# First tokens turned by the tensor engine, and score banks shared by two row tiles, in a hybrid attention layer

## Chip, cores and metric

The kernel runs on one core of one Trainium2 chip. The metric is the time of one execution in microseconds of device time; three runs of the kernel before are known.

## The reference

One layer for 2048 prompt tokens and 64 sample tokens with model width 1024. Only what the change touches is shown whole; the cache, the sample tokens and the output side are left out.

```
mod = silu(c) @ w_ada + b_ada                    # 1024 x 3072
shift, scale, gate = split(mod, 3)
h = rms_norm(x, norm_g) * (1 + scale) + shift
u = h @ w_in                                     # 1024 x 4104, split into q, k, v, z of heads A and B, f of B
qa, ka = rope(rms_norm(..)); qb, kb = rms_norm(..); logf = log_sigmoid(fb + b_f)
A: softmax(qa ka^T / 8, mask of 64-token chunks), two maps per head, a = p1 - lam * p2, a @ va
B: softmax(qb kb^T / 8 + cumulative logf bias, causal mask) @ vb
y = x + gate * (concat(A * silu(za), B * silu(zb)) @ w_out)
```

## The kernel before

**Tiling.** A block `j` is 256 tokens, two row tiles `t` = 0, 1 of 128 (row tile `i` = 2j + t); there are eight blocks and the sample block. The columns of `w_in` are cut into eight groups `g` of 512 columns, taken in the order 0, 1, 4, 5, 6, 7, 2, 3. Every product is done with operands split into an f16 high part and an f16 low part, and so costs three matmuls. `inp` computes the projection of one group and row tile (matmuls `q<-wc,hT`; `wc` are the split weights, `hT` the split and turned `h`, features on partitions). `q_evac`, `ep_*` normalise and rotate; `ep_trans` turns q and k (`tr<-ident,u`); `qk_pair` makes scores (`S<-KT,qT`); `qk_chunk` drains a score tile to `E` on VectorE; `row_*` make the softmax row and split it into `PB`; `row_trans` turns it by a DMA (`PT<-PB`); `pv` multiplies it with the values (`po<-VT,PT`).

**Start.** SP, the only queue that issues DMAs, first loads the weights of group 0 (`wc`, 2 MB), then the shift and scale columns of `w_ada` in sixteen 512 KB pieces (`wada`) with the two row tiles of block 0 (`x`) among them, then the weights of group 1. `mod_mm(hf, k)` multiplies the conditioning vectors with `wada`, first all of columns half 0, then half 1; it fills two column groups of the PSUM tile `modp`. `mod_evac` writes the result to `modr`, `mod_max` takes its maxima (`hb`), from which `sigma` makes the power of two `sig_h` that scales `h` before its split. `mod_rows` spreads `modr` over 128 partitions by matmuls, `h_first` and `h_first_split` compute and split `h` of block 0 on VectorE and ScalarE (`hl`), and `h_first_trans` turns it by four DMA transposes to `hT`. Later blocks do the same through `h_make`, `h_split` and `h_trans`, with shift and scale read back from DRAM into `shP` and `gsP`. The weights of a group are scaled by a power of two as well: `w_max` takes maxima per k (`wmx`), `w_peak` the maximum per partition, and `spread` writes the 128 numbers to DRAM (`wmx_d`) and reads them back into every partition (`wrow`); group 0 alone does this with two small matmuls (`all_max_mm`). `w_split` then makes `wc`. `warm` issues matmuls whose result nobody reads.

**Scores.** PSUM holds two score tiles `S` of 128x1024 (two banks each), one for each head of a group. `qk_pair(g, j, t, ci)` takes both for one row tile, multiplies 64-row halves of the array side by side, and adds the mask with matmuls over all 128 rows. Row tiles 0 to 3 need at most 512 columns.

**Order.** Every call is recorded with a position (`plan.event`, `ev`); `Plan` then orders the instructions of each engine: among those that could start about now it takes the one with the lowest priority number, which comes from positions, durations that the planner assumes (`cost`) and the table `SHIFT` (nanoseconds added for a kind of operation, one column for each ninth of the program). An event with `first` set goes ahead of all others. Engines run in that order and wait for each other by semaphores; a waiting instruction holds all behind it on its engine. All instructions are issued from one helper line (551).

Of the kernel before, what the change touches and what calls it, by code (L numbers as in the profile page):

```python
# [28 lines left out]
D = 1024  # L29
# [12 lines left out]
class Plan:  # L42
# [18 lines left out]
        'ep_apply DVE': (26127, -3870, -4149, 1952, -17698, -3554, -10514, -7088, -2181),  # L61
        'ep_gain POOL': (1598, 5296, 4273, 7950, 5296, 20643, 60755, 9385, 5296),
        'ep_hi ACT': (27471, 36841, 2957, 36442, -76347, -50798, 24757, 21188, 0),
        'ep_kout SP d': (-2090, 62103, 69083, 15305, -17069, 20450, 62522, 47446, -52402),
        'ep_lo DVE': (13690, 20015, 10272, -25398, 50409, 18413, 30933, 55598, 0),
        'ep_rstd POOL': (124196, -7418, -3334, -13672, 1489, -2852, -6964, -8380, 2958),
        'ep_square ACT': (1222, 7059, 69075, 100316, 33946, 17761, -559, 7791, -55499),
        'ep_square DVE': (-19737, -11205, -6053, -6235, 13891, -12021, 5467, -9194, -18777),
        'ep_square SP d': (17731, 2644, -20421, 44685, -453, 17057, 7365, -5250, -5933),
        'ep_trans PE': (-8510, 1413, 20757, 14554, 4162, -22993, -38513, -7700, 0),  # L70
        'ep_v ACT': (77357, 78843, 94474, 106969, 15393, 26795, 14839, 59051, 0),
        'ep_v DVE': (123205, 212871, 14149, 83229, 170299, 16014, -443, 779, 0),
        'f_evac ACT': (0, 283107, 0, 0, 0, 0, 0, 0, 0),
        'f_evac DVE': (0, 28121, 0, 0, 0, 0, 0, 0, 0),
        'first h0 ACT': (-47637, 0, 0, 0, 0, 0, 0, 0, 0),
        'first h0 DVE': (39992, 0, 0, 0, 0, 0, 0, 0, 0),
        'first h0 SP d': (-43600, 0, 0, 0, 0, 0, 0, 0, 0),
        'first h1 ACT': (20737, 0, 0, 0, 0, 0, 0, 0, 0),
        'first h1 DVE': (-3029, 0, 0, 0, 0, 0, 0, 0, 0),
        'first h1 SP d': (-3083, 0, 0, 0, 0, 0, 0, 0, 0),  # L80
        'first w ACT': (-1750, 0, 0, 0, 0, 0, 0, 0, 0),
        'first w DVE': (2329, 0, 0, 0, 0, 0, 0, 0, 0),
        'first w PE': (-14065, 0, 0, 0, 0, 0, 0, 0, 0),
        'first w POOL': (14606, 0, 0, 0, 0, 0, 0, 0, 0),
        'first x ACT': (-27378, 0, 0, 0, 0, 0, 0, 0, 0),
        'first x POOL': (148021, 0, 0, 0, 0, 0, 0, 0, 0),
# [9 lines left out]
        'gate_out ACT': (0, 0, 2849, 0, 0, 0, 0, 0, 0),  # L96
        'gate_out SP d': (0, 0, 77357, 0, 0, 0, 0, 0, 0),
        'gate_scale DVE': (0, 0, 0, 0, 0, 0, 0, 942, 38016),
        'h_load SP d': (-15270, 27231, 30875, 38614, 21795, -15328, 60179, -34016, 0),
        'h_make DVE': (1250, 15290, 0, 0, 0, 0, 0, 0, 0),  # L100
        'h_split ACT': (4400, 7716, 0, 0, 0, 0, 0, 0, 0),
        'h_split DVE': (-6743, 49591, 0, 0, 0, 0, 0, 0, 0),
        'h_stat ACT': (57185, -1335, 0, 0, 0, 0, 0, 0, 0),
        'h_stat POOL': (39, -11037, 0, 0, 0, 0, 0, 0, 0),
        'h_trans SP d': (2336, -121, 0, 0, 0, 0, 0, 0, 0),
        'inp PE': (-1425, -2353, -5892, 12276, 1110, 7213, 10417, 4982, 0),
        'mod ACT': (84262, 0, 0, 0, 0, 0, 0, 0, 0),
        'mod DVE': (-41547, 0, 0, 0, 0, 0, 0, 0, 0),
# [16 lines left out]
        'q_evac_s ACT': (0, 263668, 272342, 280051, 232653, 247574, 249782, 256882, 0),
        'q_evac_s DVE': (0, -32432, -42172, 30926, 8537, -46465, -66220, 99044, 0),
        'qk_chunk DVE': (-656, 14962, 14438, 14179, 33823, 12070, -8423, 32451, 24882),
        'qk_pair PE': (-686, -14880, -13186, -13282, -18376, -10584, -4934, 6105, -20805),
        'row_a_A DVE': (-4545, 35845, 81899, 0, 0, 0, 26630, 42209, 14393),
        'row_exp ACT': (239808, 30341, 63612, 112050, 254971, 49109, 107780, -3600, 161122),  # L130
        'row_hi_A ACT': (13875, -16282, 7088, 0, 0, 0, 4986, -3720, -18827),
        'row_hi_B ACT': (0, 0, 28449, 24237, 42298, 974, -14079, 0, 0),
        'row_lo_A DVE': (6455, -1845, 64402, 0, 0, 0, 42405, 45153, 41582),
        'row_lo_B DVE': (0, 0, 43352, 8756, 25691, 6871, 2028, 0, 0),
        'row_recip ACT': (5844, -78, 117755, 0, 0, 0, -69669, -12634, 71923),
        'row_recip DVE': (24207, 11431, 58294, 12857, 195542, 14343, 52846, 17171, -54082),
        'row_trans SP d': (-4043, 2148, 584, -10112, -3739, 584, 26131, 26487, 584),
        'second x ACT': (54758, 0, 0, 0, 0, 0, 0, 0, 0),
        'second x POOL': (-40204, 0, 0, 0, 0, 0, 0, 0, 0),
        'second x SP d': (-25850, 0, 0, 0, 0, 0, 0, 0, 0),  # L140
        'small ACT': (6570, 0, 0, 0, 0, 0, 0, 0, 0),
        'small DVE': (-1560, 0, 0, 0, 0, 0, 0, 0, 0),
        'small POOL': (1716, 0, 0, 0, 0, 0, 0, 0, 0),
        'small SP d': (39808, 0, 0, 0, 0, 0, 0, 0, 0),
        'smp_P ACT': (0, -75170, -26194, -12198, -25045, 28140, -35406, -31008, -38883),
        'smp_P PE': (0, -27764, -15612, -15612, -15612, -15612, -15612, -15612, -62941),
        'smp_PV PE': (0, -11187, -11670, 25841, 5585, -9507, -14440, -53633, -6031),
        'smp_S ACT': (0, -37793, -20363, -38036, 18373, 47712, -26322, 4578, -39853),
# [8 lines left out]
        'start ACT': (-58233, 0, 0, 0, 0, 0, 0, 0, 0),
        'start DVE': (47985, 0, 0, 0, 0, 0, 0, 0, 0),
        'start PE': (19278, 0, 0, 0, 0, 0, 0, 0, 0),
        'start SP d': (-2135, 0, 0, 0, 0, 0, 0, 0, 0),  # L160
        'w_coef DVE': (-9072, -20222, -33332, -11355, 19956, -7748, 16067, 0, 0),
# [1765 lines left out]
```

## Time and profile before

| | |
|---|---|
| three runs | 1624.32, 1626.23, 1629.85 us; median 1626.23 us |
| profiled execution | 1624.04 us, of it a span of 1622.3 us |
| PE busy | 1441.1 us (89%) |
| DVE (VectorE) busy | 1261.6 us (78%) |
| ACT (ScalarE) busy | 928.9 us (57%) |
| POOL (GpSimd) busy | 495.6 us (31%) |
| first matmul of the projection | 70.31 us after the span's start |

Busy time is time in which an instruction of the engine runs; a wait of PE is told with what released it. The clock columns give the granted clock of TensorE as a share of 2.4 GHz.

### The profile page before, as it was taken

To read this page: it belongs to the slowest core of one execution; us is meant where nothing else is said; L and a number is where in the kernel's file an instruction comes from. 1 tells how busy PE (TensorE), PEld (TensorE's weight loads), DVE (VectorE), ACT (ScalarE), POOL (GpSimd) and SP (SyncE) were. 2 spreads that over 40 slices of the span, in tenths; PEclk is the share of its full clock that TensorE was granted. 3 is DMA by queue.
4 is the path that set the end of the run, shared out by engine and by line. 5 is a ranking of instruction groups with operands and counts; after the bars stand their busy time and mean duration, and the time that the engine had idled before them with its cause. 6 is when DMAs were issued, how large, how long until landed. Compare 5 with 4: busy or idle time off the path is not lost. (4 is left out here: it accounts for less than half of the span.)

```text
span 1622.3 us, 29643 instructions
## 1 busy us (share of the span) xinstructions
PE 1441.1 (89%) x10900; PEld 729.1 (45%) x10900; DVE 1261.6 (78%) x2619; ACT 928.9 (57%) x1768; POOL 495.6 (31%) x620
## 2 busy tenths in 40 slices
PE   7499987888999988998889889988999899698998
PEld 3144444443454444444444444444444454344443
DVE  4588999978969886988678867986899789797431
ACT  2257765655567665775667656865665566453100
POOL 0056663324322121111212112112355354412322
PEclk9699999989999999999999999999999999899999
DMA  9758789957978899999999999999858664889772
GB/s 314 127 156 195 198 186 233 157 110 178 208 152 175 199 201 208 199 212 209 217 164 210 196 197 215 206 192 203 204 151 153 132 156 124 159 168 231 199 196 70
DMA packets 630414, 298.50 MB, mean 184 GB/s; under 512 B 513183, under 2 KB 601007, under 8 KB 623484
## 3 DMA queue, kind: packets, MB, share of 16 engines
q1 hardware_dynamic: 630268, 296.61, 85.1%
q8 instruction: 85, 1.39, 0.4%
q14 instruction: 61, 0.49, 0.1%
HBM read 129.12 MB, written 43.16 MB: 106 GB/s over the span
## 5 line engine op out<-in xcount | busy, mean ns | idle before, releaser
L551 PE MATMUL q<-wc,hT 128*128 128x512 f16 x3072 | 733.4, 383 | 27.3 <-DMA hT<-hl 17.3
L551 PEld LDWEIGHTS <-hT 128*128 128x128 f16 x3328 | 293.8, 98 | 336.6 <-issue 31.8
L551 ACT ACTIVATE E<-E,st 128x128 f32<-128x128 f32 (+15 forms) x256 | 305.9, 1196 | 158.7 <-DVE st L551 80.6
L551 PE MATMUL po<-VT,PT 128*128 128x128 f16 x3808 | 247.7, 215 | 82.3 <-DMA PT<-PB 44.6
L551 PEld LDWEIGHTS <-PT 128*128 128x128 f16 x3808 | 213.3, 100 | 154.1 <-DMA PT<-PB 69.2
L551 PE MATMUL S<-KT,qT 64*128 64x512 f16 (+3 forms) x1920 | 227.2, 355 | 17.8 <-DVE E L551 14.8
L551 DVE SCALAR_TENSOR_TENSOR PB<-E,PB 128x128 f16<-128x128 f32 (+15 forms) x128 | 164.2, 1298 | 33.7 <-ACT PB L551 32.9
L551 PE MATMUL y<-wc,ogT 128*128 128x512 f16 (+1 forms) x800 | 177.1, 380 | 2.5 <-DVE os_e L551 1.3
L551 POOL TENSOR_SCALAR rs<-rs 128x8 f32<-128x8 f32 (+1 forms) x72 | 20.6, 285 | 518.4 <-DVE rs L551 491.9
L551 ACT ACTIVATE PB<-E 128x128 f16<-128x128 f32 (+15 forms) x128 | 138.3, 1102 | 46.3 <-DMA PT<-PB 45.7
L551 DVE CUSTOM_DVE_ANT_0 E<-S,nk,cf 128x1024 f32<-128x1024 f32 (+7 forms) x128 | 131.5, 1045 | 42.6 <-PE S L551 42.4
L551 PEld LDWEIGHTS <-qT 64*128 64x128 f16 x1920 | 83.9, 95 | 143.6 <-issue 77.4
L551 DVE TENSOR_SCALAR_CACHE_REDUCE E<-S,cf 128x1024 f32<-128x1024 f32 (+7 forms) x128 | 131.4, 1042 | 13.0 <-PE S L551 12.7
L551 POOL TENSOR_TENSOR u<-u,gain 128x512 f32<-128x512 f32 (+1 forms) x72 | 96.1, 1335 | 98.1 <-DVE u L551 23.7
L551 POOL TENSOR_TENSOR rs<-rs,mhalf 128x8 f32<-128x8 f32 (+1 forms) x72 | 118.3, 1643 | 6.0
L551 PEld LDWEIGHTS <-ogT 128*128 128x128 f16 (+1 forms) x800 | 75.8, 98 | 95.9 <-issue 10.9
L551 ACT ACTIVATE u<-q,us 128x384 f32<-128x384 f32 x128 | 73.1, 572 | 75.4 <-PE q L551 37.3
L551 ACT ACTIVATE PB<-E,st 128x128 f16<-128x128 f32 (+7 forms) x64 | 76.6, 1198 | 41.1 <-DVE E L551 14.3
L551 DVE SCALAR_TENSOR_TENSOR PB<-E,st,PB 128x128 f16<-128x128 f32 (+8 forms) x64 | 87.6, 1369 | 9.7 <-ACT PB L551 9.4
L551 POOL TENSOR_TENSOR yt<-yt,xr 128x512 f32<-128x512 f32 (+1 forms) x34 | 44.0, 1295 | 142.4 <-DVE yt L551 116.0
L551 POOL TENSOR_SCALAR oar<-oar 128x1 f32<-128x1 f32 (+1 forms) x68 | 38.2, 562 | 155.6 <-ACT og L551 152.7
L551 ACT ACTIVATE og<-po,us 128x128 f32<-128x128 f32 x128 | 45.9, 359 | 60.9 <-PE po L551 51.5
(210 smaller groups left out, 1778.8 us busy)
## 6 DMA issues: line engine op xcount, KB each, us to landing
hT<-hTd SPq DMA_DIRECT2D x53, 1024.0 KB
out_dram<-u SPq DMA_DIRECT2D x128, 128.0 KB
wc<-in_w_in_dram SPq DMA_DIRECT2D x32, 256.0 KB
wada<-in_w_ada_dram SPq DMA_DIRECT2D x16, 512.0 KB
x<-in_x_prompt_dram SPq DMA_DIRECT2D x16, 512.0 KB
hTd<-hT SPq DMA_DIRECT2D x16, 512.0 KB
ogd<-og SPq DMA_DIRECT2D x64, 128.0 KB
nk<-nck_d SPq DMA_DIRECT2D x16, 512.0 KB
```

The costliest lines, as they stand in the source:

```text
L551: fn(*a, **kw)
```

## The change

1. `w_ada` is loaded in full rows k by k (eight times 1 MB) and not by column halves. `mod_mm(k)` issues four matmuls per k, into four column groups of `modp`; `mod_evac` takes all 128 partitions with one multiply-add and one maximum.
2. `h` of block 0 is turned by TensorE: ScalarE scales x by its row's reciprocal norm, sixteen f32 transposes turn it into the score tiles, and for each k VectorE applies shift and scale, now one number per partition (`mcol`, made by four transposes of `modr`), ScalarE writes the high part to `hT` and VectorE the low part. The four DMA transposes, the `mod_rows` matmuls and `hl` of block 0 go.
3. Group 1 takes its weight maximum by `all_max_mm` too, so its write to DRAM and the read back go.
4. `qk_pair` of blocks 0 and 1 makes the scores of both row tiles in one visit, in different banks of the same pair of `S` tiles.
5. `warm` matmuls are placed anew (88 at the start in the place of 90, and none of the twelve later ones), and the whole `SHIFT` table and two assumed durations are new, so that the order differs on every engine.

```diff
     SHIFT = {
-        'ep_apply DVE': (26127, -3870, -4149, 1952, -17698, -3554, -10514, -7088, -2181),
+        'ep_apply DVE': (28748, 396, -4145, 6923, -16510, 21685, -12270, -8722, -27945),
...
+    def load_ada(k):
...
+            t = st([128, 2, D], F32, f"wada{k}", tag=tag, bufs=bufs)
+            sp.dma_start(out=t.rearrange("p s c -> p (s c)"), in_=wada_v[:, k, 0:2 * D])
...
-        if g:
+        if g > 1:
             spread(g, m)
...
-        if g == 0:
-            all_max_mm(mod_ps["S0"][:, 512:1024], m[:, 0:1], m[:, 1:2])
+        if g < 2:
+            all_max_mm(O_tile() if g else mod_ps["S0"][:, 512:1024], m[:, 0:1], m[:, 1:2])
...
+        for hf in range(2):
+            for s in range(2):
+                c = 32 * (2 * hf + s)
+                pe.matmul(mod_ps["p"][c:c + 2, :], cs[:, k, :], ada_w[k][s][:, hf * 512:hf * 512 + 512], start=False, stop=(k == KC - 1))
+
+    def mod_evac():
+
+        dve.scalar_tensor_tensor(out=modr, in0=mod_ps["p"], scalar=mod1, in1=grow, op0=ALU.add, op1=ALU.mult)
+        dve.tensor_reduce(out=hb[:, 0:1], in_=modr, axis=AX, op=ALU.max, apply_absolute_value=True)
+
+    def mod_cols():
+
+        c = mod_ps["c"] = Q_tile("modc")
+        for q in range(4):
+            pe.transpose(c[:, q * 128:q * 128 + 128], modr[:, q * 128:q * 128 + 128], ident)
...
-        sp.dma_start_transpose(out=hT[0, 0][:, 8 * hf:8 * hf + 8, t * 128:(t + 1) * 128],
-                               in_=hhl[0, t][:, 4 * hf:4 * hf + 4].rearrange("p k a b -> p (k a b)"))
...
+    def h_first_x(t):
+
+        x = x_t[0, t]
+        act.activation(out=x, in_=x, func=AF.Copy, scale=hrs[0, t][:, 1:2])
+        for k in range(KC):
+            c = k % 4 * 256 + t * 128
+            pe.transpose(mod_ps[f"S{k // 4}"][:, c:c + 128], x[:, k * 128:k * 128 + 128], ident)
+
+    def h_first(k):
...
+        dve.tensor_scalar(out=x, in0=p, scalar1=mcol[:, 1, k:k + 1], scalar2=mcol[:, 0, k:k + 1], op0=ALU.mult, op1=ALU.add)
+        act.activation(out=hi, in_=x, func=AF.Copy)
+        dve.tensor_tensor(out=lo, in0=x, in1=hi, op=ALU.subtract)
...
+    for k in range(KC):
+        plan.event(-79.5 + 0.1 * k, True, "first h")
+        h_first(k)
...
+        ts = (0, 1) if j < 2 else (t,)
+        if t not in ts[:1]:
+            return
...
+    def S_cols(s, j, t):
+        return S_ps[s][:, 512 * t:512 * t + 512] if j < 2 else S_ps[s]
```

On SP, at the end of the loads, the kernel before has these rows (`wm_1` is the weight maximum of group 1, `hl_0` the split `h` of row tile 0):

```order
L551 DMA wmx_d_85<-wm_1_200 128x1
L551 DMA x_167<-in_x_prompt_dram 128x1024
L551 DMA shP<-mod_d 128x1024
L551 DMA wrow_201<-wmx_d_85 128x128
L551 DMA_TRANSPOSE hT_0_176<-hl_0_175 128x8x128 x2
L551 DMA gsP<-mod_d 128x1024
```

and the changed kernel these (`x_173` is block 1):

```order
L547 DMA mod_d<-modr 2x512 x4
L547 DMA wc_120<-in_w_in_dram 128x4x128
L547 DMA x_173<-in_x_prompt_dram 128x1024 x2
L547 DMA shP<-mod_d 128x1024
L547 DMA gsP<-mod_d 128x1024
L547 DMA x_0_239<-in_x_prompt_dram 128x1024
```

The write and read of the maxima and the transposes are gone from between the loads, and `gsP` is loaded directly behind `shP`.

On VectorE, the changed kernel has these rows where the last low part of block 0 is done and the maximum of group 1 (`wm_1`, with the matmuls into `po`) is still to be made; before, the maximum was read from `wrow`:

```order
L547 TENSOR_TENSOR hT_0_172<-x_1_153,hT_0_172 128x256 x2
L547 TENSOR_REDUCE wmx_199<-wc_115 128x1
...
L547 TENSOR_REDUCE wmx_199<-wc_120 128x1
L547 TENSOR_REDUCE wm_1_200<-wmx_199 128x1
L547 SCALAR_TENSOR_TENSOR x_173<-x_173,hr_0_175,gsP 128x1024
L547 TENSOR_REDUCE wm_1_200<-po 1x1
L547 TENSOR_TENSOR x_173<-x_173,shP 128x1024
L547 COPY wm_1_200<-po 128x1
```

Six of the eight `w_max` of group 1 now stand behind the first `h`, and the two passes over x of block 1, which read `gsP` and `shP`, stand between the steps of the maximum.

On TensorE, the changed kernel makes the scores of both row tiles of block 0 in one piece (the first visit of group 0; `S_0_0` and `S_0_1` are the two tiles):

```order
L547 MATMUL S_0_0_0_231<-KT_0_221,qT_0_222 128x128
L547 LDWEIGHTS qT_0_222
L547 MATMUL S_0_1_0_232<-KT_0_221,qT_0_222 128x128
L547 LDWEIGHTS qT_0_222
L547 MATMUL S_0_0_0_231<-KT_0_221,qT_0_222 128x256
L547 LDWEIGHTS qT_0_222
L547 MATMUL S_0_1_0_232<-KT_0_221,qT_0_222 128x256
...
L547 MATMUL S_0_1_0_232<-mask_b_100,ident_b 128x64
L547 LDWEIGHTS hT_1_216
L547 MATMUL q_1_0_224<-wc_126,hT_1_216 128x512
```

Before, the 128-column and the 256-column scores stood in two visits with projection matmuls between them; behind the one visit now come the last four k of a projection.

## Rows read from the trace of the kernel before

**Rows 1.** Busy time by stretch: us, then engines, clock, DMA share, GB/s.
```profile
14.00:38.00 24.00, 21.14 (x101) 7.03 (x99) 16.59 (x33) 7.84 (x13) 2.40 (x12) 0.94 1.04 389
38.00:42.00 4.00, 4.00 (x11) 0.52 (x12) 0.69 (x1) 0.00 (x0) 0.00 (x0) 0.50 1.06 235
54.00:66.00 12.00, 0.96 (x3) 0.58 (x3) 7.16 (x18) 3.82 (x6) 0.74 (x2) 0.50 0.80 41
70.00:80.00 10.00, 9.69 (x50) 4.12 (x51) 6.79 (x29) 4.66 (x8) 0.00 (x0) 0.68 0.79 168
```

**Rows 2.** Timeline of the SP queue: start us, length us, what.
```profile
28.39 0.37 SPq L551 DMA_DIRECT2D wada<-in_w_ada_dram  x1
54.89 0.35 SPq L551 DMA_DIRECT2D wmx_d<-wm  x1
55.82 0.37 SPq L551 DMA_DIRECT2D shP<-mod_d  x1
63.01 0.32 SPq L551 DMA_DIRECT2D wrow<-wmx_d  x1
63.42 5.73 SPq L551 DMA_TRANSPOSE hT<-hl  x2
```

**Rows 3.** Timeline of PE from the modulation to block 1.
```profile
38.60 8.79 PE L551 MATMUL modp<-wada,cs 128*2 128x512 f32 x30
54.01 0.37 PE L551 MATMUL mod<-ident,hb 128*2 128x128 f32 x1 [4.08 <-DVE hb L551]
70.31 1.03 PE L551 MATMUL q<-wc,hT 128*128 128x512 f16 x2 [14.49 <-DMA hT<-hl]
95.78 0.66 PE L551 MATMUL tr<-ident,u 128*128 128x128 f32 x4 [0.68 <-POOL u L551]
96.35 0.59 PE L551 MATMUL q<-wc,hT 128*128 128x512 f16 x2
```

**Rows 4.** Timeline of PE's weight loads in the modulation.
```profile
18.29 0.08 PEld L551 LDWEIGHTS modp<-bada,ones 1*2 1x2 f32 x2 [0.21 <-issue]
19.23 0.09 PEld L551 LDWEIGHTS modp<-wada,cs 128*2 128x2 f32 x2 [0.86 <-issue]
...
26.27 0.09 PEld L551 LDWEIGHTS modp<-wada,cs 128*2 128x2 f32 x2 [0.34 <-issue]
26.69 0.09 PEld L551 LDWEIGHTS modp<-wada,cs 128*2 128x2 f32 x2 [0.34 <-issue]
```

**Rows 5.** Timeline of VectorE, 53 to 98 us.
```profile
53.98 0.69 DVE L551 TENSOR_REDUCE wmx<-wc 128x1 f32<-128x512 f32 x1
56.23 0.22 DVE L551 TENSOR_SCALAR sig_h<-sig_h_e 128x1 int32<-128x1 int32 x2
69.25 0.29 DVE L551 TENSOR_REDUCE wm<-wrow 128x1 f32<-128x128 f32 x1 [7.94 <-DMA wrow<-wmx_d]
80.43 0.75 DVE L551 SCALAR_TENSOR_TENSOR wc<-wc,us,wc 128x512 f16<-128x512 f32 x1 [1.36 <-ACT wc L551]
85.22 1.28 DVE L551 SCALAR_TENSOR_TENSOR x<-x,hr,gsP 128x1024 f32<-128x1024 f32 x1
92.03 0.68 DVE L551 TENSOR_TENSOR u<-u,rs 128x512 f32<-128x512 f32 x1
97.26 0.48 DVE L551 SCALAR_TENSOR_TENSOR KT<-tr,sg,KT 128x256 f16<-128x256 f32 x1
```

**Rows 6.** Timeline of PE around a visit of `qk_pair` with 256 columns.
```profile
125.47 0.38 PE L551 MATMUL q<-wc,hT 128*128 128x512 f16 x1
125.77 0.50 PE L551 MATMUL S<-KT,qT 64*128 64x256 f16 x6
126.21 0.23 PE L551 MATMUL S<-mask_b,ident_b 128*128 128x64 bf16 x2
126.28 0.60 PE L551 MATMUL q<-wc,hT 128*128 128x512 f16 x2
126.71 0.20 PE L551 MATMUL qf<-wc,hT 128*128 128x16 f16 x2
```

**Rows 7.** Waits of PE from 100 us on: total, times, longest.
```profile
PE po L551 <- DMA PT<-PB: 44.6, 32, 6.1
PE S L551 <- DVE E L551: 14.8, 14, 7.5
```

More of the change, by code (lines that the diff above doesn't have):

```diff
@@ L157 @@
[L157 to L161, printed above, removed]
-        'w_coef POOL': (11122, 0, 0, 0, 0, 10141, 9150, 0, 0),
-        'w_load SP d': (1568, -13268, -10100, 20125, 22689, -53853, 40583, 0, 0),
-        'w_max DVE': (6726, 82742, 70908, 125915, -40677, -24609, 23494, 0, 0),
@@ new lines @@
+        'first h DVE': (-3578, 0, 0, 0, 0, 0, 0, 0, 0),
+        'first w ACT': (-58489, 0, 0, 0, 0, 0, 0, 0, 0),
+        'first w DVE': (166953, 0, 0, 0, 0, 0, 0, 0, 0),
+        'first w PE': (14802, 0, 0, 0, 0, 0, 0, 0, 0),
+        'first w POOL': (-10121, 0, 0, 0, 0, 0, 0, 0, 0),
+        'first x ACT': (888, 0, 0, 0, 0, 0, 0, 0, 0),
+        'first x PE': (459, 0, 0, 0, 0, 0, 0, 0, 0),
+        'first x POOL': (-11545, 0, 0, 0, 0, 0, 0, 0, 0),
[9 rows of a table added]
+        'gate_out ACT': (0, 0, 44671, 0, 0, 0, 0, 0, 0),
@@ new lines @@
+        'second x ACT': (57333, 0, 0, 0, 0, 0, 0, 0, 0),
+        'second x POOL': (-36654, 0, 0, 0, 0, 0, 0, 0, 0),
+        'second x SP d': (-37489, 0, 0, 0, 0, 0, 0, 0, 0),
+        'small ACT': (85370, 0, 0, 0, 0, 0, 0, 0, 0),
+        'small DVE': (-900, 0, 0, 0, 0, 0, 0, 0, 0),
+        'small POOL': (88770, 0, 0, 0, 0, 0, 0, 0, 0),
+        'small SP d': (67896, 0, 0, 0, 0, 0, 0, 0, 0),
+        'smp_P ACT': (0, -130836, -160843, -170685, -130171, 29403, -119445, -117083, -133383),
+        'smp_P PE': (0, 67629, -59638, -64536, -66745, -64689, -65139, -62866, -65823),
@@ L663, in hybrid_layer_kernel @@
     sp.dma_start(out=cst, in_=consts[:, 0:384])
+    dve.memset(grow, 1.0)
     for hf in range(2):
@@ L853, in hybrid_layer_kernel @@
     hb = st([128, 8], F32, "hb")
-    dve.memset(hb, 2.0 ** -46)
-    def mod_mm(hf, k):
-        for s in range(2):
-            c, o = 32 * (2 * hf + s), s * D + hf * 512
-            if k == 0:
-                pe.matmul(mod_ps["p"][c:c + 2, :], ones[0:1, 0:2], bada[0:1, o:o + 512], start=True, stop=False)
-            pe.matmul(mod_ps["p"][c:c + 2, :], cs[:, k, :], ada_w[4 * hf + k // 2][k % 2][:, s, :], start=False, stop=(k == KC - 1))
-    def mod_evac(hf):
-        a, b = slice(64 * hf, 64 * hf + 2), slice(64 * hf + 32, 64 * hf + 34)
-        p = mod_ps["p"]
-        act.activation(out=modr[a, :], in_=p[a, :], func=AF.Copy)
-        dve.scalar_tensor_tensor(out=modr[b, :], in0=p[b, :], scalar=1.0, in1=grow[b, :], op0=ALU.add, op1=ALU.mult)
@@ L869, in mod_max @@
-    def mod_max(hf):
-        for s in range(2):
-            a = slice(64 * hf + 32 * s, 64 * hf + 32 * s + 2)
-            dve.tensor_reduce(out=hb[a, s:s + 1], in_=modr[a, :], axis=AX, op=ALU.max, apply_absolute_value=True)
-    def mod_rows(hf):
-        for s in (1, 0):
-            c = 64 * hf + 32 * s
-            p = mod_ps[hf, s] = mod_ps[f"S{s}"][:, 0:512] if hf == 0 else Q_tile(f"mod{2 + s}")
-            plan.event(plan.pos + 0.1, name="mod")
-            pe.matmul(p, ident[c:c + 2, c:c + 1].broadcast_to([2, 128]), modr[c:c + 2, :], start=True, stop=True)
@@ L882, in mod_store, with mod_mm @@
-    def mod_store(hf):
-        for s in range(2):
-            c = 64 * hf + 32 * s
-            sp.dma_start(out=mod_d[:, s, hf * 512:hf * 512 + 512], in_=modr[c:c + 2, :])
+    mod1 = st([128, 1], F32, "mod1")
+    dve.memset(mod1, 0.0)
+    for hf in range(2):
+        dve.memset(mod1[64 * hf + 32:64 * hf + 64], 1.0)
+    mcol = st([128, 2, KC], F32, "mcol")
+    def mod_mm(k):
+        for hf in range(2):
+            for s in range(2):
+                c, o = 32 * (2 * hf + s), s * D + hf * 512
+                if k == 0:
+                    pe.matmul(mod_ps["p"][c:c + 2, :], ones[0:1, 0:2], bada[0:1, o:o + 512], start=True, stop=False)
+        for hf in range(2):
+            for s in range(2):
+                c = 32 * (2 * hf + s)
+                pe.matmul(mod_ps["p"][c:c + 2, :], cs[:, k, :], ada_w[k][s][:, hf * 512:hf * 512 + 512], start=False, stop=(k == KC - 1))
@@ new lines, in mod_evac, with mod_store @@
+    def mod_evac():
[5 more added lines that the diff above has]
+            pe.transpose(c[:, q * 128:q * 128 + 128], modr[:, q * 128:q * 128 + 128], ident)
+    def mod_store():
+        for hf in range(2):
+            for s in range(2):
+                c = 64 * hf + 32 * s
+                sp.dma_start(out=mod_d[:, s, hf * 512:hf * 512 + 512], in_=modr[c:c + 2, :])
@@ L1008, in hybrid_layer_kernel @@
     mod_ps["S0"], mod_ps["S1"] = S_tile("mod0"), S_tile("mod1")
-    NW = 8
-    for k in range(NW):
+    dve.memset(mod_ps["p"], 0.0)
+    for k in range(KC):
         w_load(0, k)
     f_load()
-    for n in range(8):
-        load_ada(n)
-        if n in (3, 5):
-            x_load(0, (n - 3) // 2)
-    for k in range(NW, KC):
-        w_load(0, k)
+    for k in range(KC):
+        load_ada(k)
+        if k in (3, 5):
+            x_load(0, (k - 3) // 2)
     plan.event(-100, name="first w")
@@ L1029, in hybrid_layer_kernel @@
     h_stat(0, 1)
-    for hf in range(2):
-        for k in range(KC):
-            plan.event(-96 + 8 * hf + k)
-            mod_mm(hf, k)
-            if 8 * hf + k >= WARM0:
-                plan.event(-95.5 + 8 * hf + k)
-                warm(3)
-        plan.event(-95.5 + 8 * hf + 7, name="mod")
-        mod_evac(hf)
-        mod_max(hf)
-        mod_rows(hf)
-        mod_store(hf)
-    for n in range(WARM1):
-        plan.event(-80 + 0.1 * n)
-        warm(3)
-    plan.event(-79, name="second x")
+    for k in range(KC):
+        plan.event(-96 + 2 * k)
+        mod_mm(k)
+        plan.event(-95 + 2 * k)
+        warm(WARM0)
+        if k in (4, 6):
+            plan.event(-95 + 2 * k + 0.5, name="first x")
+            h_first_x((k - 4) // 2)
+    plan.event(-80.5, True, "mod")
+    mod_evac()
+    mod_cols()
+    hmix = st([1, 128], F32, "hmix", tag="rt", bufs=1)
+    dve.memset(hmix, 34.0)
+    hp = Q_tile("modh")
+    plan.event(-80)
+    warm(WARM1)
+    plan.event(-79.9, True, "mod")
+    pe.transpose(hp[0:1, 0:128], hb[:, 0:1], ident)
+    dve.tensor_reduce(out=hb[0:1, 2:3], in_=hp[0:1, 0:128], axis=AX, op=ALU.max)
+    plan.event(-79.8)
+    warm(WARM1)
+    plan.event(-79.7, True, "mod")
+    pe.matmul(hp[:, 128:129], hmix, hb[0:1, 2:3], start=True, stop=True)
+    dve.tensor_scalar(out=hb[:, 4:5], in0=hp[:, 128:129], scalar1=2.0 ** -46, scalar2=None, op0=ALU.max)
+    sig_h = sigma(hb[:, 4:5], "sig_h", floor=False)
+    dve.tensor_scalar(out=mcol.rearrange("p s (h q) -> p s h q", h=2),
+                      in0=mod_ps["c"].rearrange("p (q h s r) -> p s h q r", q=4, h=2, s=2)[:, :, :, :, 0],
+                      scalar1=sig_h[:, 0:1], scalar2=None, op0=ALU.mult)
+    plan.event(-79.6)
+    warm(2 * WARM1)
+    for k in range(KC):
+        plan.event(-79.5 + 0.1 * k, True, "first h")
+        h_first(k)
+    plan.event(-70, name="second x")
+    mod_store()
     mod_load(0)
@@ L1050, in hybrid_layer_kernel @@
             h_stat(j, t)
-    plan.event(-70, name="mod")
-    hmix = st([2, 128], F32, "hmix", tag="rt", bufs=1)
-    dve.memset(hmix, 33.0)
-    dve.memset(hmix[0:1, :], 1.0)
-    hp = mod_ps["S1"][:, 512:1024]
-    pe.transpose(hp[0:2, 0:128], hb[:, 0:2], ident)
-    dve.tensor_reduce(out=hb[0:2, 2:3], in_=hp[0:2, 0:128], axis=AX, op=ALU.max)
-    pe.matmul(hp[:, 128:129], hmix, hb[0:2, 2:3], start=True, stop=True)
-    dve.tensor_copy(hb[:, 4:5], hp[:, 128:129])
-    sig_h = sigma(hb[:, 4:5], "sig_h", floor=False)
-    for t in range(2):
-        plan.event(-70, name=f"first h{t}")
-        for hf in range(2):
-            h_first(t, hf)
-        for hf in range(2):
-            h_first_split(t, hf)
-            h_first_trans(t, hf)
     plan.event(-50, name="small")
```

261 lines of the change are left out of this document (119 added, 142 removed), and 31 rows, old and new, of the table SHIFT.

## The prediction

> **What bounds the kernel now.** I read the page first, for the shares: PE is busy 89% of the span, VectorE 78%, so PE is the engine to look at. Then the busy time by stretch, to see where PE idles: between 54 and 66 us it has 0.96 us of work and stands at half clock, while DMA moves 41 GB/s [rows 1]. Third, PE's own timeline: the first projection matmul starts at 70.31 us, after a wait of 14.49 us for the DMA transposes of `h` [rows 3]. Nothing later in the program has a wait of that size; from 100 us on the largest sum is 44.6 us, over 32 waits for turned softmax rows [rows 7]. So the start is a serial chain, and what follows is a stream in which PE seldom stops.
>
> The chain, from the end: the transposes are issued at 63.42 us, although `sig_h` is ready at about 56.4 us and the first half of `hl` soon after. SP stood at the read of `wrow`, which waits for the 512 bytes written to `wmx_d` at 54.89 us and is issued only at 63.01 us [rows 2, 5]. Ahead of that the second half of the modulation ran on PE until 47.4 us, continuously for 8.79 us [rows 3]; the loads were done well before: DMA holds 389 GB/s from 14 to 38 us and falls to 235 GB/s when only the narrow rows of `wc` are left [rows 1], so the last `wada` lands at about 38.5 us (24 us at 389 GB/s are 9.3 MB, against 9.4 MB of `wada` and x).
>
> **The change, step by step.**
>
> *Modulation.* The bytes are the same and in the same order up to the last `wada` [rows 2], so it lands at 38.5 us again. Only the four matmuls of k = 7 are then left. Rows 4 tell what such a matmul costs: two that follow each other in one column group start 0.94 us apart (18.29 and 19.23), two that alternate between two groups 0.42 us (26.27 and 26.69) [rows 4]. With pairs side by side k = 7 takes 4 x 0.42 = 1.7 us at full clock and 3.4 us at half, with four side by side half of either. I take 1.7 us, which is pairs at full clock or fours at half; bounds 0.9 and 3.4. The modulation ends at 40.2 us, against 47.4.
>
> By the Trainium skill (TensorEngine Tiling (Array Packing), Theoretical Speedup), a stationary operand of at most 32 columns can run up to four tiles at once. No row here has four; by that rule k = 7 would take 0.9 us at full clock and the forecast below would be 0.8 us lower, by pairs at half clock it would be 1.7 us higher.
>
> *To the first product.* `mod_evac` is two passes of 512 columns, each like the 0.69 us of a reduction of that width [rows 5]: 41.6 us. From there the old chain runs unchanged: it took from 54.01 (transpose of `hb`, [rows 3]) to 56.45 (`sig_h`, [rows 5]), 2.4 us. One `w_max` of 0.69 us stands in between in the new order and can delay it, which gives 44.7 us, and `mcol` 0.2 more (the length of the two `sig_h` operations): 44.9 us. k = 0 needs one VectorE pass over 128x256 from PSUM, 0.48 us by the same shape in `KT` [rows 5], and a ScalarE pass of the same width, taken as the same: about 45.9 us. The first projection matmul moves from 70.31 to about 46, 24 us earlier. No DMA stands in that path any more.
>
> *What paces block 0 after that.* PE would take 25.5 us for block 0 in both groups (70.31 to 95.78, [rows 3]), so from 46 it could be at block 1 by 71.5. But VectorE now has more in its queue. Sixteen passes of the first `h` at up to 0.48 us take it from 44.9 to about 52.3; then six `w_max` at 0.69, 4.1 us, and some 0.6 us of small ones: 57.0. Then the maximum of group 1: its two matmuls on PE hide behind the two passes over x of block 1 (1.28 us each at most, [rows 5]), together 3.2 us to the copy of `wm_1`: 60.2. In the kernel before the same point is 69.54 (69.25 + 0.29), and from there to the pass that normalises u of group 0 (92.03) it takes 22.5 us [rows 5]. From this list the new order has taken out the two passes over x (2.5 us) and put one split of 1.28 us behind it; and VectorE was idle in it, mostly for ScalarE's half of `w_split` (1.36 us before one of them, [rows 5]), 3.2 us in 70 to 80 [rows 1], which falls away as there is now other work to do. 22.5 - 2.5 - 1.3 - 3.2 = 15.5, so that the pass ends its wait at 75.7 and not 92.03: **16.3 us** earlier. The turning of u and the projection of block 1 hang on it by GpSimd (the wait of 0.68 us at 95.78 names it, [rows 3]) and come 16.3 us earlier as well: at about 80 us. Bounds: 13 if VectorE's idle time is not filled, 19 if the six `w_max` find room while VectorE waits for ScalarE.
>
> *Score banks.* A visit of `qk_pair` costs PE more than its columns: the last projection matmul before it starts at 125.47, and a 512-column matmul follows the next by 0.22 us at this clock (126.71 - 126.28 is two of them), so it is through at 125.69; the next projection starts at 126.28 [rows 6]. Of these 0.59 us, 3 x 256 columns and 2 x 64 at 2.4 GHz are 0.37, so 0.22 us are the change to row halves and back. Two visits less per group and eight groups are 16 x 0.22 = **3.5 us**. PE is the busiest engine, so I take it whole. The second visit also no longer waits until the first's tiles are drained; that is part of the 14.8 us of waits for `E` [rows 7], of which I take a tenth, **1.5 us**; bounds 0 and 5.
>
> *At nothing.* The transposes of x (16 on PE) run while PE waits for `wada`; if they came after the last, they would add some 2 us (four take 0.66, [rows 3]). The `memset`s at the start lie before the first weights land. Fewer `warm` matmuls leave the clock as low at the first product as it is now (0.50 in 54 to 66, [rows 1]), so that the slow first projections cost the same as before.
>
> *The order of the rest* has new numbers everywhere. No row prices it; I take 0, with bounds of a quarter of the waits of rows 7, some 15 us either way.
>
> **Sum.** 16.3 + 3.5 + 1.5 = 21.3 us. Against the profiled execution's own 1624.04 this gives 1602.7. The median of the runs lies 2.2 us higher, the lowest run 0.3; for the median of the new kernel I forecast **1603.5 us**, chance 0.52, with a range of its own of 1597 to 1609.
>
> **Rivals.**
>
> *Late inputs of block 1.* The pass over x of block 1 stands in VectorE's queue in front of the maximum of group 1 and needs `gsP` and `shP`, rows broadcast to 128 partitions. The one broadcast that the trace shows alone is bad: from the issue of `shP` at 55.82 DMA moves 41 GB/s until 66 [rows 1, 2]. If the broadcast itself is slow, 1 MB issued at about 46 lands at 60 to 66 and holds up `w_split` and PE by 3 to 9 us. Against it: the same stretch has the 128 writes of 4 bytes to `wmx_d`, and SP's wait of 8 us for them [rows 2] makes these the likelier cause; they are gone. Time 1609; chance 0.16.
>
> *Modulation on PE's clock.* If four column groups are no faster than two and the clock stays at half between the pieces, k takes 3.4 us, more than the 2.7 us in which 1 MB comes at 389 GB/s [rows 1], and PE ends at 47 as before. Start at 53, VectorE's queue 7 us later: 21.3 - 7 = 14.3 us gained, 1610; chance 0.09. For it speaks the clock of 0.50 in 38 to 42 [rows 1], with PE busy on nothing but these matmuls.
>
> *The new order also saves waits later*: a third of the 44.6 us for turned rows [rows 7] makes 1589; chance 0.11.
>
> *Other side: the score tiles are held too long.* A merged visit frees the two tiles only after four drains by VectorE and not two, at 0.48 to 0.75 us each (256 and 512 columns by the nearest rows, [rows 5]), so the next scores can come 1.0 to 1.5 us later at 16 places; if each also waits the mean of today's waits for `E`, 14.8 / 14 = 1.06 us [rows 7], 16 x 2.6 = 41 us are lost, and the kernel is slower at 1644. From 1.3 us a place the gain is gone. Against it: behind the visit shown in the order stand projections, which need no `S`. Chance of slower 0.06; a lower price that just eats the gain (1621 to 1631) 0.06.
>
> **How the numbers follow.** A measurement of this kernel tells 0.3%, 4.9 us, from no change. Faster: 0.52 + 0.16 + 0.09 + 0.11 = 0.88; same 0.06; slower 0.06. The range reaches from the bound of the order's saving (1603.5 less 13) up to the two rivals at 1609 and 1610 with the lower bound of 13 us for the start: 1590 to 1615; it leaves out 0.12 above and some 0.08 below.
>
> **What the new profile would show.** The last matmul on `modp` at about 40 us; `sig_h` near 44.7; the first projection matmul near 46 and not later than 48, with VectorE as its releaser and no DMA; projections of group 1 paced by `w_split` until about 78; the matmuls of block 1 near 80. Each visit of blocks 0 and 1 is twelve score matmuls in one piece. It is wrong if the first projection starts at 46 but block 1 at 85 or later (first rival), if `modp` ends near 47 (second), or if the waits for `E` on `S` grow beyond 30 us (last).

## The result and the profile after

| | before | after |
|---|---|---|
| median of the runs | 1626.46 us (4 runs) | 1582.92 us (4 runs, 1581.57 to 1586.43) |
| span of the profiled execution | 1622.3 us | 1579.9 us |
| PE busy | 1441.1 us | 1424.7 us |
| mean granted clock | 0.966 | 0.974 |

The ratio is 0.9734, with a 95% interval of 0.9710 to 0.9758: 43.5 us faster, where 21.3 us were forecast. The time lies below the predicted range, and below the rival of 1589.

Where it came from is read first by cutting both programs at the first matmul of block 1, which PE starts at 96.35 us before [rows 3] and at 77.04 us after. The windows up to there and from there, first of the kernel before (stretch, its length, busy time of PE, PEld, DVE, ACT and POOL, granted clock, DMA share, GB/s):

```profile
0.00:96.35 96.35, 66.44 (x320) 27.22 (x321) 54.46 (x152) 27.47 (x46) 9.69 (x27) 0.84 0.84 218
96.35:1622.30 1525.95, 1374.63 (x10581) 701.86 (x10579) 1207.11 (x2467) 901.47 (x1723) 485.91 (x593) 0.97 0.86 182
```

and of the changed kernel:

```profile
0.00:77.04 77.04, 56.04 (x322) 25.50 (x323) 49.91 (x151) 31.36 (x54) 11.81 (x30) 0.88 0.85 263
77.04:1579.90 1502.86, 1368.62 (x10581) 701.02 (x10579) 1212.33 (x2474) 901.15 (x1718) 496.21 (x591) 0.98 0.86 184
```

So 19.3 us of the 42.4 us of span are won before block 1, and 23.1 us behind it, by the same number of PE's instructions (10,581): PE is idle there for 1502.86 - 1368.62 = 134.2 us in the place of 151.3 (17.1 less), and busy 6.0 us less, at a granted clock of 0.98 and not 0.97.

**The start.** PE's timeline of the changed kernel (start us, length us, and in brackets the idle time before and its releaser; compare [rows 3, 6]):

```profile
17.35 1.04 PE L547 MATMUL modp<-wada,cs 128*2 128x512 f32 x8
28.95 1.89 PE L547 MATMUL modp<-wada,cs 128*2 128x512 f32 x8 [1.87 <-DMA wada<-in_w_ada_dram]
37.34 1.58 PE L547 MATMUL modp<-wada,cs 128*2 128x512 f32 x8
43.68 1.03 PE L547 MATMUL q<-wc,hT 128*128 128x512 f16 x2 [2.03 <-ACT hT L547]
58.73 0.39 PE L547 MATMUL q<-wc,hT 128*128 128x512 f16 x1 [0.66 <-ACT wc L547]
72.14 1.89 PE L547 MATMUL q<-wc,hT 128*128 128x512 f16 x8 [0.41 <-DVE wc L547]
76.20 1.04 PE L547 MATMUL tr<-ident,u 128*128 128x128 f32 x4 [2.18 <-POOL u L547]
77.04 1.06 PE L547 MATMUL q<-wc,hT 128*128 128x512 f16 x2
```

The modulation ends at 37.34 + 1.58 = 38.92 us, the first projection follows at 43.68 with ScalarE's high part as its releaser and no DMA, and group 1's projection is paced by the split weights `wc`. VectorE on that path (compare [rows 5]):

```profile
38.97 0.75 DVE L547 SCALAR_TENSOR_TENSOR modr<-modp,mod,grow 128x512 f32<-128x512 f32 x1 [10.17 <-PE modp L547]
42.10 0.21 DVE L547 TENSOR_SCALAR sig_h<-sig_h_e 128x1 int32<-128x1 int32 x2
42.29 0.23 DVE L547 TENSOR_SCALAR mcol<-modc,sig_h 128x16 f32<-128x16 f32 x1
49.10 0.88 DVE L547 TENSOR_TENSOR hT<-x,hT 128x256 f16<-128x256 f32 x2
53.36 0.68 DVE L547 TENSOR_REDUCE wmx<-wc 128x1 f32<-128x512 f32 x1
54.28 1.28 DVE L547 SCALAR_TENSOR_TENSOR x<-x,hr,gsP 128x1024 f32<-128x1024 f32 x1
56.81 0.14 DVE L547 COPY wm<-po 128x1 f32<-128x1 f32 x1
70.58 0.68 DVE L547 TENSOR_TENSOR u<-u,rs 128x512 f32<-128x512 f32 x1
```

The pass over x of block 1 (54.28) has no wait in front of it, although SP issues the two broadcasts that it needs only at these times (the SP queue, compare [rows 2]):

```profile
46.78 0.33 SPq L547 DMA_DIRECT2D shP<-mod_d  x1
47.20 0.38 SPq L547 DMA_DIRECT2D gsP<-mod_d  x1
```

**The rest.** PE's waits from 80 us to the end (total us, times, longest; compare [rows 7]):

```profile
PE po L547 <- DMA PT<-PB: 44.3, 35, 4.4
PE po L547 <- DVE og L547: 17.3, 18, 2.2
PE tr L547 <- POOL u L547: 15.1, 12, 2.6
PE S L547 <- DVE E L547: 13.8, 11, 8.9
```

The two sums that the forecast spoke of have hardly moved (44.6 to 44.3 us, 14.8 to 13.8 us). The gain behind block 1 is in no one of them. A good part of it lies in waits that the kernel before has once to three times and the changed kernel has hardly or not at all. In the kernel before, from 100 us on, these are among them:

```profile
PE q L551 <- DVE g L551: 6.6, 1, 6.6
PE sP L551 <- DVE sE L551: 5.5, 3, 5.0
PE po L551 <- DVE E L551: 4.2, 1, 4.2
```

In the changed kernel the first of these sums is 2.2 us, the second 0.2, and the third does not occur: 13.9 us less. Other waits became shorter or longer by up to 4 us each. Nor does the lead grow steadily. By the start of the matmul with which PE reaches a given share of the projection's 3,200 matmuls of 512 columns, it is 27 us at the first, 18 us at 10% (162 and 145 us), 31 us at 20% (309 and 278), 33 us at 50% (730 and 697), 45 us at 80% (1142 and 1096) and 41 us at the last (1386 and 1346). One place where it grows is the single wait of 6.6 us of the kernel before, between 10% and 20%:

```profile
255.76 1.01 PE L551 MATMUL q<-wc,hT 128*128 128x512 f16 x2 [6.58 <-DVE g L551]
```

In the changed kernel no wait of PE from 140 to 272 us is longer than 1.7 us.

### The profile page after: what moved, and what is told of

It reads as the page before. It is cut to its first block, busy times and chain, and to the rows that moved or that the text cites. A ratio compares the mean times of both kernels' runs of the same rounds, so it can differ in the third digit from the quotient of the medians.

```text
span 1579.9 us, 29641 instructions
## 1 busy us (share of the span) xinstructions
PE 1424.7 (90%) x10901; PEld 726.5 (46%) x10901; DVE 1262.2 (80%) x2624; ACT 932.5 (59%) x1772; POOL 508.0 (32%) x620
## 5 line engine op out<-in xcount | busy, mean ns | idle before, releaser
L547 ACT ACTIVATE E<-E,st 128x512 f32<-128x512 f32 (+15 forms) x256 | 305.9, 1196 | 155.1 <-DVE st L547 82.9
L547 PE MATMUL po<-VT,PT 128*128 128x128 f16 x3808 | 241.8, 214 | 71.8 <-DMA PT<-PB 44.3
L547 PEld LDWEIGHTS <-PT 128*128 128x128 f16 x3808 | 209.7, 99 | 144.8 <-DMA PT<-PB 61.4
L547 PE MATMUL S<-KT,qT 64*128 64x512 f16 (+3 forms) x1920 | 223.8, 352 | 24.2 <-DVE E L547 13.8
L547 DVE SCALAR_TENSOR_TENSOR PB<-E,PB 128x128 f16<-128x128 f32 (+15 forms) x128 | 165.5, 1302 | 42.4 <-ACT PB L547 42.0
L547 POOL TENSOR_TENSOR u<-u,gain 128x512 f32<-128x512 f32 (+1 forms) x72 | 100.1, 1391 | 116.5 <-DVE u L547 20.2
L547 DVE SCALAR_TENSOR_TENSOR PB<-E,st,PB 128x128 f16<-128x128 f32 (+7 forms) x64 | 88.5, 1382 | 9.9 <-ACT PB L547 9.5
L547 POOL TENSOR_TENSOR yt<-yt,xr 128x512 f32<-128x512 f32 (+1 forms) x34 | 51.4, 1514 | 120.3 <-DVE yt L547 84.6
L547 POOL TENSOR_SCALAR oar<-oar 128x1 f32<-128x1 f32 (+1 forms) x68 | 31.8, 467 | 152.5 <-ACT og L547 149.4
```

What stands on the lines that cost most here:

```text
L547: fn(*a, **kw)
```

## The experiments

The trials ran on a chip on which both kernels take 0.5 to 0.8% longer, so each is told by its ratio to the kernel before on the same chip; the changed kernel, unaltered, was run there too.

> The changed kernel unaltered, on the chip of the trials: 0.971 to 0.976 if ratios carry over from chip to chip, as they have been read so far. At 0.967 or below the trials' distance to it, the order's share above all, would be larger by 10 us than told.

Measured 0.9737 (0.9711 to 0.9762): ratios carry over.

**1. The start put back, in an unchanged order.** Pieces of the modulation's weights are loaded twice, all of them or the first four (the edit shown); every other instruction keeps its place.

```diff
             for fn, a, kw in o.calls:
+                if o.dma and any(n in kw["out"].tensor.name for n in ("wada0", "wada1", "wada2", "wada3")):
+                    fn(*a, **kw)
                 fn(*a, **kw)
```

> The changed kernel in its own order, but each piece of w_ada is loaded twice, 8.4 MB more before the modulation: the first projection is to start some 22 to 30 us later than 43.7 (8.4 MB at 389 GB/s and the waits of each second load for the first). If a delay of the start passes on whole, the end moves by what the first projection of block 1 (77.0) moves. If later stages are set by something else than the start, the end moves by clearly less than that.

> The changed kernel in its own order, with the first four of the modulation's pieces of weights loaded twice, which should move the first projection matmul from 43.7 to about 62 to 65 us and block 1 from 77 to about 96, where it was before the change. If the start is worth its 19 us and the order the rest: 0.9734 + 19/1626 = 0.985, with 0.983 to 0.988 for a delay of 17 to 23 us. If the early start were also the cause of the lead that grows later (rival): 0.995 or more.

With all of them the first projection starts at 88.82 us, 45.1 later than after, where 22 to 30 were expected, and block 1 at 125.41, 48.4 later; the ratio is 1.0012 (0.9991 to 1.0033): 0.0278 x 1626.5 = 45 us lost. With four, PE's timeline has

```profile
62.49 1.04 PE L549 MATMUL q<-wc,hT 128*128 128x512 f16 x2 [2.03 <-ACT hT L549]
97.80 0.59 PE L549 MATMUL q<-wc,hT 128*128 128x512 f16 x2
```

and the ratio is 0.9862 (0.9823 to 0.9902): 0.0128 x 1626.5 = 20.8 us lost for a first projection 18.8 us later and a block 1 that comes 97.80 - 77.04 = 20.8 us later. The intervals leave some 5 to 8 us either way, so the agreement to a tenth is chance; within them a delay of the start is passed on one to one. So the 19.3 us are worth about 19 us, and the rest keeps its gain with a late start: a program that reaches block 1 1.4 us after the kernel before is still 1.4% (1.0 to 1.8%) faster than it. The rival, that the lead later on grows out of the early start, falls.

**2. Tables exchanged, and the merge undone.** The kernels are put together from three parts: the start (with its `warm` matmuls and assumed durations), the merged `qk_pair`, and the table `SHIFT` (the old, the new, or empty). Kinds of operation that only one of the two starts has stand in its own table alone, and have no number under the other. Undoing the merge means the old `qk_pair`:

```diff
-        ts = (0, 1) if j < 2 else (t,)
-        if t not in ts[:1]:
-            return
+        i = 2 * j + t
```

> The changed kernel with the old visits (one row tile each, its own pair of score tiles), the new numbers of the planner kept; the order of the rest shifts with it. My step: 5 us lost (3.5 for the changes, 1.5 for waits on drained tiles), 1588. Rival, the merge is where the unforeseen 21 us lie: 1604 to 1609. Rival, any shift of the order costs: numbers drawn for one program do not fit another, 1595 or more, without a clear place in the trace.

> The changed kernel with the planner's old table (the kinds that only the new start has get none). If the start and the merge are worth 19 + 5 us and the new numbers the other 19, this runs at about 1602. If the start is worth all 43 us by itself, about 1583 to 1588. If numbers that do not belong to a program cost more than none at all, above 1605.

> The kernel before (old start, two visits of score banks) with the new table of numbers. If a table is worth something only with the program that it was made for: slower than before by 15 to 45 us (ratio 1.010 to 1.028), as the old table in the changed kernel gave the whole gain away. If the new numbers are better whatever the program is (rival): faster by some 20 us, the part of the gain that the start does not explain (0.987). The start must stay where it was: first projection matmul near 70 us, since the two chains ahead of it do not depend on the table.

> The new start alone: two visits of score banks and the old table. The first projection matmul near 44 us and block 1 near 77 to 81 either way. If the merge does nothing by itself and a table without its program costs some 20 to 40 us: ratio 0.99 to 1.01, within 10 us of the changed kernel with the old table (0.9991). If the merge saves 20 us by itself (rival, from the 22 us that undoing it cost): 1.012, 20 us above that kernel. If the old table still fits two visits, and only the merge had spoiled the fit: 0.985 to 0.99, which is the start's 19 us alone.

> The merged visits alone, in the old start with the old table. If the merge has a price of its own of -9 us (as with the tables at 0: 1.0066 against 1.0009): 0.994 or so. If its sign comes from the order that it meets: with the old table in the new start it cost 15 us (0.9899 against 0.9991), so 1.005 to 1.015 here.

For the empty table:

```diff
-    SHIFT = {
-        'ep_apply DVE': (28748, 396, -4145, 6923, -16510, 21685, -12270, -8722, -27945),
...
+    SHIFT = {}
```

> The changed kernel with every number of the table set to 0, so that the order comes from the planner's rules alone. Read against the kernel before with its table at 0 as well. If the structure is worth the start and nothing else: 15 to 25 us less than that kernel, the lead being there at block 1 and neither growing nor falling beyond some 15 us after it. If the merged visits or the earlier inputs save all along (rival): 35 us or more less. Both are slower than 1626 us; by how much, 50 to 200 us, no row tells.

> The kernel before with every number of the table set to 0. First projection matmul near 70 us as before. By the theory of the start alone 15 to 25 us more than the changed kernel with its table at 0, by the rival 35 us or more. That both lie 50 us or more above 1626 would say that the tables carry more time than the change of the start does.

> The new start with two visits of score banks and the table at 0; it stands between the kernel before with the table at 0 (1.0164) and the changed kernel with the table at 0 (1.0009). If the start carries the difference and the merge nothing: 0.998 to 1.004. If the merge carries a part of it (rival: undoing the merge cost 22 us with the new table): 1.008 to 1.014.

Ratios to the kernel before (95% intervals of 0.0015 to 0.0035 either way):

| start, `qk_pair` | old table | new table | empty table |
|---|---|---|---|
| old, two visits | 1 | 1.0126 | 1.0164 |
| new, two visits | 0.9899 | 0.9868 | 1.0066 |
| old, merged | 1.0053 | | |
| new, merged | 0.9991 | 0.9734 | 1.0009 |

Read by rows: the same program takes from 0.9734 to 1.0009 by its table alone, 45 us, with the same work and nearly the same start (block 1 at 78.46 us with the new, 80.80 with the old and 81.79 with the empty table). The new table makes the old program 20 us slower, and the old table takes the whole gain from the new one. So the new numbers are not better in themselves. Read by columns: the new start gains in each, 16 us with the old and with the empty table and 42 us with the new. That is not the start alone: block 1 comes 17.7 us earlier under the new table (79.46 against 97.14) and 8.2 us under the empty one (87.40 against 95.60); the rest of these gains arises behind it. The merge costs 15 us with the old table in the new start and 8.6 us in the old start, and gains 22 us with the new table and 9 us with the empty one (the differences in the table, times 1626 us). The sign of the merge is set here by the order that it meets. The empty tables were expected to run 50 to 200 us longer than 1626; they run 1 and 27 us longer than the kernel before.

PE's waits in the old program with the new table show where the misfit appears:

```profile
PE po L547 <- DMA PT<-PB: 67.9, 36, 14.2
PE S L547 <- DVE E L547: 26.4, 15, 9.5
```

Both sums are larger than those of [rows 7] by half or more, 35 us together, for the same instructions; the whole kernel loses 20 us. Without the merge, under the new table, the first of them is 63.8 us over 44 waits.

**3. The table scaled.** Every number of a kernel's own table times 0.95, 1.02 or 1.05; the work is the same.

```diff
-        return self.SHIFT[o.kind][min(max(int(o.pos // 9), 0), 8)] if o.kind in self.SHIFT else 0.0
+        return self.SHIFT[o.kind][min(max(int(o.pos // 9), 0), 8)] * 0.95 if o.kind in self.SHIFT else 0.0
```

> The changed kernel with every number of its table taken times 0.95: work, sizes and start as they are, only the order a little different. If the new table's gain is a fit to single places of this program, which any shift of the order loses: slower than the changed kernel (0.9734) by 8 us or more, at 0.978 to 0.995. If it is a good coarse order that small shifts leave alone (rival): within 5 us, 0.970 to 0.977.

> The changed kernel with every number of its table times 1.02. By the theory of a fit to single places: between 0.975 and 0.99, nearer to 0.9734 than 1.05 (0.985) was, if the time goes smoothly with the shift; anywhere in 0.975 to 1.005 if each shift is a new draw. By the rival of a good coarse order, now unlikely: 0.970 to 0.975.

> The same with every number times 1.05: by the theory of the fit 0.978 to 0.995 again, by the rival 0.970 to 0.977. A side on which it becomes faster than 0.970 would say that the table is no best point at all.

> The kernel before with every number of its own table times 0.95. By the theory of the fit slower than before by 8 to 35 us, 1.005 to 1.020, towards the 1.0164 of its table at 0; by the rival within 5 us of 1.

> The kernel before with every number of its table times 1.05: 0.9974 was measured at 0.95. If the old table is a point from which shifts lose only a little: 0.997 to 1.008; if it is a tuned point like the new one: 1.01 to 1.03.

| table times | 0.95 | 1 | 1.02 | 1.05 |
|---|---|---|---|---|
| changed kernel | 1.0040 | 0.9734 | 0.9870 | 0.9850 |
| kernel before | 0.9974 | 1 | | 1.0111 |

All three scalings of the changed kernel lose, 19 to 50 us, and not in the order of the scaling: 1.02 loses no less than 1.05. They behave like new draws and not like steps away from a best point. One single place of the worst draw is on PE's timeline, before the last block's output:

```profile
1607.87 30.63 PE L547 MATMUL y<-wc,ogT 128*128 128x512 f16 x128 [17.76 <-DMA ogT<-oghl]
```

Of the 51.0 us by which this span (1645.3 us) is longer than that of the changed kernel on the same chip (1594.3 us), 17.8 are this one wait. There, in the changed kernel, PE runs the output without one:

```profile
1471.57 115.94 PE L547 MATMUL y<-wc,ogT 128*128 128x512 f16 x536 [0.98 <-DVE os_e L547]
```

The kernel before is itself no best point: 0.95, by the theory of a fit 8 to 35 us slower, makes it 4 us faster.

**4. The change to row halves, by itself.** In a merged visit the first row tile gets its mask before the second's scores, so that the array changes once more to row halves and back in each of the 16 visits. The order is the changed kernel's.

```diff
-        for n, (a, b) in enumerate(((0, 0), (0, 1), (1, 0))):
-            for t in ts:
+        for t in ts:
...
+            for n, (a, b) in enumerate(((0, 0), (0, 1), (1, 0))):
```

> The changed kernel with every instruction in its place, except that a merged visit finishes row tile 0 with its mask before row tile 1 begins, so that the array changes between whole and half rows once more in each of 16 visits. If a change costs what the rows of before show, 0.22 us, this adds 3.5 us to 1582.9: 1586.4. If merging is worth more by the array's changes alone (rival: the unexplained 21 us lie here, 1.3 us a visit), it comes to about 1604. If the changes hide, 1583.

> The merged visits with one more change to row halves and back in each of 16, the order as it is. By the forecast's 0.22 us each 3.5 us more than the changed kernel, 0.0022 in the ratio; if such a change costs nothing, within 1.5 us (0.001) of it.

The visit itself got longer as forecast. In the changed kernel, on the chip of the trials, it is:

```profile
82.67 0.38 PE L547 MATMUL q<-wc,hT 128*128 128x512 f16 x1
...
82.98 0.67 PE L547 MATMUL S<-KT,qT 64*128 64x128 f16 x12
83.58 0.29 PE L547 MATMUL S<-mask_b,ident_b 128*128 128x64 bf16 x4
83.71 0.60 PE L547 MATMUL q<-wc,hT 128*128 128x512 f16 x2
```

and with one more change:

```profile
79.60 0.38 PE L547 MATMUL q<-wc,hT 128*128 128x512 f16 x1
...
79.91 0.34 PE L547 MATMUL S<-KT,qT 64*128 64x128 f16 x6
80.18 0.23 PE L547 MATMUL S<-mask_b,ident_b 128*128 128x64 bf16 x2
80.34 0.50 PE L547 MATMUL S<-KT,qT 64*128 64x256 f16 x6
80.78 0.23 PE L547 MATMUL S<-mask_b,ident_b 128*128 128x64 bf16 x2
80.84 0.60 PE L547 MATMUL q<-wc,hT 128*128 128x512 f16 x2
```

From one projection matmul to the next 1.24 us stand against 1.04: 0.20 us for one change, where 0.22 were worked out from [rows 6]. But the time of the whole kernel was 0.9731 (0.9709 to 0.9753), and 0.9738 (0.9719 to 0.9758) beside the changed kernel's 0.9737: nothing of the 16 x 0.2 = 3.2 us is seen in it. The intervals of some 0.002 either way are as wide as that sum, so a part of it is not excluded; what is shown is a price at the visit and none that could be measured at the end.

The Trainium skill (TensorEngine Tiling (Array Packing), Key Properties) says that a change of the tiling mode drains TensorE, without a price; the rows of the visit fit this, at 0.20 us a change to halves and back; that it is a drain no row shows.

## Why the prediction was wrong

The sign, the mechanism and the path of the start were right; the size was off by 21 us: 3 us of it at the start, the other 18 behind block 1, where one term stood at nothing.

**The failed step: "The order of the rest has new numbers everywhere. No row prices it; I take 0, with bounds of a quarter of the waits of rows 7, some 15 us either way."** Behind block 1 the forecast had this 0 and 5.0 us for the merged visits; the two together measured 23.1 us in the profile, and 1.4% of the kernel in experiment 1, where the start was as late as before. If the merge gave its 5.0, the order gave 18; no run separates them. Both the value and the bound were wrong, the bound first: tables for the same program lie 45 us apart (experiment 2), and a scaling by a few per cent moves the time by 4 to 50 us (experiment 3). A quarter of two groups of waits cannot hold that, since the order sets the waits of every group, the single long ones (6.58 us before, 17.76 us in a bad draw) too. The predicted range did not even keep that bound: it reached only 13 us below the forecast. The sign could not be read from the rows of before. The rival "the new order also saves waits later" had the right place but put it on the turned rows, whose waits have not changed (44.6 and 44.3 us), and its time of 1589 was still too high.

**The modulation**: right, with a term that was too large. It ends at 38.9 us, forecast 40.2. The four matmuls of k = 7 took 1.58 us, taken as 1.7, but by PE's weight loads that holds a wait for the last piece of `wada`:

```profile
37.88 0.10 PEld L547 LDWEIGHTS modp<-wada,cs 128*2 128x2 f32 x6 [0.46 <-DMA wada<-in_w_ada_dram]
```

From there to the end the other three took 1.04 us at a granted clock of 1.00, as long as four side by side at 17.35 and near the lower bound of 0.9. The rival on PE's clock fell, although the granted clock was 0.50 in between (1.89 us for the four matmuls at 28.95): PE still kept up with the loads.

**To the first product**: right, 43.68 us against 46. Its releaser was ScalarE and not VectorE. From the last `modp` to `mcol` (42.52) it took 3.6 us and not 4.7: from the transpose of `hb` (40.50) to `sig_h` (42.31) 1.8 us stand in the place of 2.4 and 0.69. Two `w_max` (40.36 and 41.15) run in that stretch, mostly while VectorE waits for PE.

**What paces block 0**: right by its mechanism, 19.3 us against 16.3, just above the upper bound of 19. VectorE ended the sixteen passes at 49.98 (forecast 52.3), the `w_max` at 54.04 (57.0), copied `wm` at 56.81 (60.2) and normalised u at 70.58 (75.7). Of the 21.4 us won by that pass (92.03 before) 2.1 were lost again, nearly all on GpSimd, whose gain and rotation took 4.7 us (71.40 to 76.14) in the place of 2.9 (92.85 to 95.73). Its timeline after:

```profile
71.40 1.82 POOL L547 TENSOR_TENSOR u<-u,gain 128x512 f32<-128x512 f32 x1 [7.35 <-ACT wc L547]
73.30 2.00 POOL L547 TENSOR_TENSOR rt<-u,ropeP 128x128 f32<-128x128 f32 x3
75.69 0.45 POOL L547 TENSOR_TENSOR u<-rt 128x128 f32<-128x128 f32 x1
```

and before:

```profile
92.85 1.26 POOL L551 TENSOR_TENSOR u<-u,gain 128x512 f32<-128x512 f32 x1 [1.45 <-DVE u L551]
94.19 1.00 POOL L551 TENSOR_TENSOR rt<-u,ropeP 128x128 f32<-128x128 f32 x3
95.28 0.45 POOL L551 TENSOR_TENSOR u<-rt 128x128 f32<-128x128 f32 x1
```

**Late inputs of block 1**: the rival fell. The broadcasts issued at 46.78 and 47.20 kept nothing waiting at 54.28.

**Score banks**: the price of the change to row halves was right (0.20 and 0.22 us), the 3.5 us that were made of it were not found in the time; "PE is the busiest engine, so I take it whole" took a cost on PE for a cost of the program, though PE is idle for 134 us behind block 1 even now. The waits for `E` fell by 1.0 us, forecast 1.5. What the merge does to the time beyond that could not be told apart from the order: its sign turns with the table.

**Score tiles held too long** (the other side): not seen as forecast, the waits for `E` are 13.8 us. With the old table the merge does raise them, from 17.8 to 25.0 us in the new start and from 14.8 to 25.7 us in the old one, where it costs 15 and 8.6 us; with the empty table it lowers them from 24.7 to 22.8 us. That fits the mechanism in an order that was not made for the merge, at 7 to 11 us and not at 41; that the later release of the tiles causes these waits was not tested.

What stays open: how the 23 us divide between the merge and the order, which of the new numbers carry them, and whether the kernel before, with a table of its own that fits as well, would have them too. No run here searched for one.

## What to carry to other kernels

A start that is a serial chain is worth what it is shortened by: delays of block 1 by 21 and 48 us cost 21 and 45 us, one to one within the intervals. A table of priorities has to be priced as a term of its own, by what other tables do to the same program: empty, scaled by a few per cent, or exchanged. Where that spread is larger than the edit, a trial that undoes one edit under one table measures the misfit together with the edit (the merge: 22 us gained, 9 gained or 15 lost in the new start); compare under several tables or in one fixed order.

## What the runs showed of the hardware

Four matmuls of 512 f32 columns in four column groups take 1.04 us together at a granted clock of 1.00 (17.35) and 1.89 us at 0.50 (28.95), where [rows 4] have 0.94 us for each of those that follow each other in one group. The forecast's 1.7 us left open whether fours gain over pairs. By the Trainium skill (TensorEngine Tiling (Array Packing), Theoretical Speedup) up to four such tiles run at once, and the trace agrees.

GpSimd's three `rt` products took 2.00 us after and 1.00 us before for the same shapes, and its gain 1.82 and 1.26 us. All of the first difference is in one product of 128x128, 1.45 us from 73.30 against 0.45 us. It began while VectorE ran this pass, and ended 0.3 us after it:

```profile
73.16 1.27 DVE L547 SCALAR_TENSOR_TENSOR hl<-x,sig_h,hl 128x1024 f16<-128x1024 f32 x1
```

Before, VectorE ran only instructions of one column beside that product. So the delay went with a long pass on VectorE; whether that is the cause was not tested.
